# An encoder trunk on one core: the pooling projection third in the mixer, the Fourier projection up, the first gate/up pairs laid out by hand, and RMSNorm factors as columns

## The chip, the cores and the metric

The kernel runs on one core of a Trainium2 chip. Five engines of that core work side by side, each through its own instructions in order: PE (TensorE, matrix products into PSUM), DVE (VectorE), ACT (ScalarE), POOL (GpSimd) and SP (SyncE, which here only issues transfers). They wait for one another by semaphores. The metric is the device time of one execution in microseconds (us), as the median of three runs.

## What is computed

The reference is a two-layer bidirectional encoder on x of 512 positions by 1024 channels in float32:

```python
for l in range(2):
    x = x + 0.5 * swiglu(rmsnorm(x, g1), w_gate, w_up, w_down)      # hidden width 2816
    p = rmsnorm(x, g2) @ w_in          # 256 pool, 256 Fourier, 3 x 512 attention channels
    y_pool = mean pooling (windows 2, 4, 8, 16) minus the token, a 64x64 map per group, a scale
    y_four = Re(fft2 over positions and 64 channels of a group) @ fourier_w
    y_attn = softmax(q1 k1 + alibi) v - lam * softmax(q2 k2 + alibi) v, RMSNorm per head
    x = x + concat(y_pool, y_four, y_attn) @ w_out
    x = x + 0.5 * swiglu(rmsnorm(x, g3), ...)
return rmsnorm(x, g_final)
```

## The kernel before

**Tiling.** x lies transposed in SBUF as eight tiles `x0` to `x7`, 128 channels by 512 positions. Each fp32 product is made of three fp32r matmuls (`mm3`: high x high, high x low, low x high), since a value is kept as a high part `hi` (rounded by ACT) and a low part `lo` (the rest, by DVE); `split` (L102 to L104) makes both. Weights come in as `st` tiles of 512 KB on SP's queue; `operand` hands out the next pair `hi`, `lo`, always AHEAD = 3 operands early, and numbers them in the order of use (`hi139` is the high part of operand 139).

**The feed-forward parts.** 22 row blocks are worked in 11 units of two. A `Unit` is a 2x2 block product by seven products instead of eight (Strassen's scheme in Winograd's form), so its weights and inputs are sums: some sums of weights are made by a second, accumulating transfer on POOL's queue into an `st` tile that has been split already. `head` makes the products `qe` and `qa`, `middle` `qb`, `qg`, then `y`, `v` and `w` (L436 to L438) on DVE and the rest of `qa`, and waits for the norm's factor; `tail`, called after the next unit's head, adds a product to `qg` once `w` has read it, and another to `qe`. A `dn` product per channel tile follows after every 4, 4 and 3 units. The very first unit is a `FirstUnit`: it makes all eight products, as it starts from plain tiles that are there early; the lines that call `plain` for it stand at the end of `build` (L819 to L828).

**Norms.** The products run on x times the gain (`xh`, `xl`), and each result is multiplied by the factor 1/rms later. For the factor, ACT squares the eight tiles, POOL adds six of the squares up (L288), DVE the last; a matmul with ones adds over the partitions (`total`), and nine DVE instructions of 128x512 (`rsqrt`) make the factor, the same in all partitions. The last norm (`Final`) does it otherwise: `columns` has four one-column matmuls give the sums of 4 x 128 positions as a 128x4 tile, the nine instructions run on 128x4, and `dg` (diagonal blocks) with four matmuls spreads the factor over the partitions (`r`, L387).

**The mixer.** Steps named in the string `ORDER` run as listed there: `P0` to `P3` (query and key projections), `N` (factor), `E0` to `E3` (their splits), `Shq` (scores of head h, block q: a max on DVE, an exponential on ACT, a combination on DVE), `T` (transposes), `V0`, `V1`, `VE` (values), `X`, `Y` (attention output), `A` and `F` (pooling and Fourier projections), `AE0`, `AE1` (window sums on DVE), `PD`, `PL0`, `PL1` (pooling maps on PE), `FE0`, `FE1` (folds of the Fourier half on DVE), `FG`, `FD`, `TB`, `GH` (its maps), `W0a` to `W3` (output projection). Each engine's list is a single queue: an instruction that waits holds up all that is behind it on that engine. A scheduler may move instructions of different steps past each other; the lists that result are shown below.

## Time and profile before

| | |
|---|---|
| median of three runs | 1855.18 us (1854.42 to 1856.44) |
| profiled execution, its own time | 1856.4 us |
| its span in the trace | 1854.4 us |
| busy PE, DVE, ACT, POOL | 1767.0, 1314.8, 884.8, 250.0 us |
| mean granted TensorE clock | 0.986 |

The span runs from the first to the last instruction of the trace; 2.0 us of the execution lie around it. PE is busy for 95% of it, so what can be changed by another order is the time in which PE waits, the time in which it runs at half the clock, and the work that it is given. The trace tells of each instruction its start, its length and, in brackets, how long its engine stood idle before it and what ended that.

### The profile page before, as it was taken

What the parts mean: (1) busy time and instruction counts of PE and PEld (TensorE: products, weight loads), DVE (VectorE), ACT (ScalarE), POOL (GpSimd) and SP (SyncE); (2) the same over time, 40 slices, a digit from 0 to 9 for tenths busy, and PEclk for the clock granted to TensorE, in tenths of its full rate; (3) what the DMA queues carried; (4) which work ended last, traced back from release to release, by engine and by line L of the source; (5) the groups of instructions that cost most, each with busy time, mean ns of one, the idle gap of its engine ahead of it and who ended that gap; (6) DMA issues with size and microseconds to landing.
All of it is one profiled execution on the core that took longest, in us unless ns stands there. A gap on an engine that the chain in (4) does not pass through costs nothing.

```text
span 1854.4 us, 28082 instructions
## 1 busy us (share of the span) xinstructions
PE 1767.0 (95%) x11249; PEld 1600.8 (86%) x11249; DVE 1314.8 (71%) x1962; ACT 884.8 (48%) x1225; POOL 250.0 (13%) x272
## 2 busy tenths in 40 slices
PE   7899999999798999999989999999987989999997
PEld 7889989877677889989889899898776888899896
DVE  6865856878679774856898467477877897567474
ACT  6433524468656433524554244244975554244243
POOL 1101101111103101101130010102111210010101
PEclk9899999999999999999999999999999999999998
DMA  8656857454625757857578586675444566586561
GB/s 250 146 159 152 202 137 165 142 139 126 143 65 131 174 152 160 202 138 165 155 156 206 127 197 167 135 173 160 116 118 106 106 147 186 125 195 170 132 164 46
DMA packets 81347, 279.70 MB, mean 151 GB/s; under 512 B 9152, under 2 KB 12224, under 8 KB 81216
## 3 DMA queue, kind: packets, MB, share of 16 engines
q0 software_dynamic: 29376, 106.97, 33.2%
q1 hardware_dynamic: 48672, 167.26, 27.7%
q10 hardware_dynamic: 3168, 3.68, 0.6%
q8 instruction: 88, 1.44, 0.3%
q14 instruction: 43, 0.35, 0.1%
HBM read 258.99 MB, written 2.10 MB: 141 GB/s over the span
## 4 chain that ended last, share of the span: by engine, by line
PE 77%; DVE 8%; ACT 6%; DMA 5%; issue 2%; POOL 0%; SPq 0%; ACTq 0%; DVEq 0%; POOLq 0%
PE dn L107 8%; PE dn L108 7%; PE dn L109 7%; PE qg L420 4%; DMA st<-in_gu 4%; PE qg L421 4%; PE qg L422 4%; PE qe L420 4%; PE qe L421 4%; PE qe L422 4%; PE qa L422 4%; PE qa L421 4%; PE qa L420 4%; DVE lo L104 2%; PE qb L421 2%
## 5 line engine op out<-in xcount | busy, mean ns | idle before, releaser
L103 ACT ACTIVATE hi<-st 128x1024 fp32r<-128x1024 f32 (+2 forms) x420 | 433.1, 1036 | 645.7 <-PE dn L108 218.1
L104 DVE TENSOR_TENSOR lo<-st,hi 128x1024 fp32r<-128x1024 f32 (+2 forms) x420 | 503.5, 1202 | 182.9 <-ACT hi L103 179.8
L108 PE MATMUL dn<-al,hi 128*128 128x512 f32 x704 | 274.6, 390 | 0.0
L109 PE MATMUL dn<-ah,lo 128*128 128x512 f32 x704 | 274.1, 389 | 0.0
L107 PE MATMUL dn<-ah,hi 128*128 128x512 f32 x704 | 272.0, 392 | 0.6
L420 PE MATMUL qg<-xh,hi 128*128 128x256 f32 x688 | 197.4, 287 | 8.7 <-DVE w L438 7.6
L181 POOL DMA_DIRECT2D st<-in_gu x129 | 116.1, 900 | 648.9 <-DVE lo L104 558.5
L421 PE MATMUL qg<-xh,lo 128*128 128x256 f32 x688 | 196.7, 286 | 0.0
L422 PE MATMUL qg<-xl,hi 128*128 128x256 f32 x688 | 196.7, 286 | 0.0
L420 PE MATMUL qe<-xh,hi 128*128 128x256 f32 x608 | 173.4, 285 | 14.5 <-ACT xh L103 8.0
L518 DVE SCALAR_TENSOR_TENSOR x<-dn,x 128x512 f32<-128x512 f32 x96 | 66.2, 689 | 164.7 <-PE dn L109 164.6
L421 PE MATMUL qe<-xh,lo 128*128 128x256 f32 x608 | 172.5, 284 | 2.1 <-DVE lo L104 2.1
L422 PE MATMUL qe<-xl,hi 128*128 128x256 f32 x608 | 172.3, 283 | 1.9 <-DVE xl L104 1.8
L107 PEld LDWEIGHTS dn<-ah,hi 128*128 128x128 f32 x704 | 131.3, 188 | 32.5 <-ACT ah L103 6.5
L108 PEld LDWEIGHTS dn<-al,hi 128*128 128x128 f32 x704 | 132.2, 188 | 28.7 <-DVE al L104 2.4
L109 PEld LDWEIGHTS dn<-ah,lo 128*128 128x128 f32 x704 | 132.2, 188 | 26.7
L420 PEld LDWEIGHTS qg<-xh,hi 128*128 128x128 f32 x688 | 134.0, 195 | 9.5 <-DVE w L438 8.0
L421 PEld LDWEIGHTS qg<-xh,lo 128*128 128x128 f32 x688 | 134.1, 195 | 0.0
L422 PEld LDWEIGHTS qg<-xl,hi 128*128 128x128 f32 x688 | 134.0, 195 | 0.0
L420 PEld LDWEIGHTS qe<-xh,hi 128*128 128x128 f32 x608 | 116.7, 192 | 17.8 <-ACT xh L103 8.8
L420 PE MATMUL qa<-xo,hi 128*128 128x256 f32 x424 | 121.0, 285 | 5.4 <-ACT q L429 5.4
L422 PE MATMUL qa<-xo,hi 128*128 128x256 f32 x424 | 121.3, 286 | 2.8 <-DVE xo L104 2.8
(270 smaller groups left out, 4099.9 us busy)
## 6 DMA issues: line engine op xcount, KB each, us to landing
st<-in_gu SPq DMA_DIRECT2D x176, 512.0 KB, 4.5
st<-in_gu POOLq DMA_DIRECT2D x172, 512.0 KB, 5.6
st<-in_dn SPq DMA_DIRECT2D x64, 512.0 KB, 3.9
lo<-st POOLq DMA_DIRECT2D x32, 512.0 KB, 5.2
st<-in_dn SPq DMA_DIRECT2D x32, 384.0 KB, 3.2
st<-in_qk SPq DMA_DIRECT2D x16, 512.0 KB, 3.7
st<-in_wo SPq DMA_DIRECT2D x16, 512.0 KB, 3.7
st<-in_wv SPq DMA_DIRECT2D x8, 512.0 KB, 4.4
```

The source lines that it names most:

```text
L103: A.activation(hi, src, AF.Copy)
L104: (lo_eng or V).tensor_tensor(lo, src, f(hi), SUB)
L107: T.matmul(o, lh, rh, start=start, stop=False)
L108: T.matmul(o, lh, rl, start=False, stop=False)
L109: T.matmul(o, ll, rh, start=False, stop=stop)
L181: G.dma_start(t[:, 0:w], then, accum_op=ADD)
L420: T.matmul(o, wh[:, s], xh, start=start and p == 0 and z == 0, stop=False, **k)
L421: T.matmul(o, wl[:, s], xh, start=False, stop=False, **k)
L422: T.matmul(o, wh[:, s], xl, start=False, stop=stop and p == NK - 1 and z == 1, **k)
L518: V.scalar_tensor_tensor(X[m], b, 0.5, X[m], MUL, ADD)
```

## The change

- `ORDER`: projection `A` is now third (after `P1`), its window sums `AE0`, `AE1` follow `E0`, `E1` and `P2`, and `PD`, `PL0`, `PL1` lie among the scores. `F` takes the old place of `A` (after `Y1`), and `FE0`, `FE1` come ahead of the scores `S31`, `S33`; `FG0` and `FG1` both come ahead of `W1a`.
- All norms: the squares are added by DVE alone. The factor is made on 128x4 columns as in `Final`, and spread over the partitions by one fp32 matmul of 512 columns (`spread`; ACT copies it to SBUF). In the mixer the spread stands inside `P1`, after 24 of its 48 matmuls, and `VE` takes the columns as they are, so the four transposes `rb` go. `Final` spreads by the one matmul too.
- The first two units: `begin` lists them by hand. The first weights come in four parts, interleaved with the plain tiles; half of the even x tiles come on ACT's transfer queue; the second unit begins with `qa` on an operand that needs no sum (the recipes change for it), then `qe`, `qg`, `qb`; the squares stand after the sums; the first unit's first results are copied out of PSUM. Eight warming matmuls instead of five.

```diff
@@ -50,10 +50,10 @@
 SLOPES = [2.0 ** (-8.0 * (h + 1) / NH) for h in range(NH)]
 NT = S // 2 + 2
 NG = 54
-NWARM = 5
+NWARM = 8
 ORDER = (
-    "P0 N L P1 E1 P2 E0 S01 S11 S13 E2 V0 S03 S00 S10 S12 S22 S02 S21 T0 V1 GD VE TD T1 X0 S23 S20 Y0 P3 "
-    "T2 PD X1 E3 Y1 A GH S30 S32 AE0 AE1 F PL0 X2 S31 S33 PL1 FE0 T3 W0a FE1 Y2 FG0 W1a FG1 TB X3 FD1 FD0 "
+    "P0 N L P1 A E0 E1 AE0 P2 AE1 S01 S11 S13 E2 PD V0 S03 S00 S10 PL0 S12 S22 S02 PL1 S21 T0 V1 GD VE TD T1 X0 "
+    "S23 S20 Y0 P3 T2 X1 E3 Y1 F GH S30 S32 FE0 FE1 X2 S31 S33 T3 W0a Y2 FG0 FG1 W1a TB X3 FD1 FD0 "
     "Y3 W0b W1b W2 W3"
 ).split()
...
@@ -140,6 +140,11 @@
                             continue
                         t, t11 = raw(a21, plus=a22), raw(a11)
                         t12, t22 = raw(a12), raw(a22)
+                        if u == 1 and i == 0:
+                            for x, then in ((t11, a21), (t, a11), (t11, None), (t, a12), (t12, None)):
+                                operand_of(x, then=then)
+                            tail = [(t22, None), (t, None)]
+                            continue
...
@@ -196,10 +209,10 @@
         sm = cp.tile([P, NSMALL], F32, name="sm")
         nc.sync.dma_start(sm, small)
         X = [cp.tile([P, S], F32, name=f"x{k}") for k in range(KT)]
-        load(1)
+        load(1, NK)
         for c in range(2):
             for k in range(0, KT, 2):
-                nc.sync.dma_start(X[k][:, c * TH : (c + 1) * TH], xt[k][:, c * TH : (c + 1) * TH])
+                (nc.sync if c else nc.scalar).dma_start(X[k][:, c * TH : (c + 1) * TH], xt[k][:, c * TH : (c + 1) * TH])
         load(2)
...
@@ -265,9 +277,27 @@
             T.matmul(b, ones, lo, start=False, stop=True)
             return b
 
+        one = cp.tile([P, 1], F32, name="one")
+        V.memset(one, 1.0)
+
+        def columns(sq):
+
+            b = bank("ss")
+            for i in range(4):
+                T.matmul(b[:, i : i + 1], sq[:, i * P : (i + 1) * P], one, start=True, stop=True)
+            return b[:, 0:4]
+
+        def spread(y):
+
+            r, dg = bank("r"), g(name="dg")
+            for i in range(4):
+                V.tensor_scalar(dg[:, i * P : (i + 1) * P], ident, y[:, i : i + 1], None, MUL)
+            T.matmul(r, onef, dg, start=True, stop=True)
+            return r
+
         class Norm:
             def __init__(self, c):
-                self.c, self.h, self.l, self.acc, self.r = c, {}, {}, None, None
+                self.c, self.h, self.l, self.acc, self.col, self.r = c, {}, {}, None, None, None
 
             def feed(self, k):
...
@@ -279,19 +309,34 @@
                 V.tensor_scalar(self.h[k], X[k], gain, None, MUL)
                 V.scalar_tensor_tensor(self.l[k], X[k], gain, f(self.h[k]), MUL, SUB)
 
-            def squared(self, k, eng=G):
+            def square(self, k):
                 sq = g(name="sq")
                 A.activation(sq, X[k], AF.Square)
+                return sq
+
...
                     self.acc = sq
                 else:
-                    (V if k == KT - 1 else eng).tensor_tensor(self.acc, self.acc, sq, ADD)
+                    V.tensor_tensor(self.acc, self.acc, sq, ADD)
+
+            def squared(self, k):
+                self.add(self.square(k))
+
+            def factor(self):
+                v = col(4, "nv", 2)
+                V.tensor_scalar(v, columns(self.acc), -0.5 / D, -0.5 * EPS, MUL, ADD)
+                self.col = rsqrt_of(v, False, 4)
+
+            def spread(self):
+                self.r = g(name="r")
+                A.activation(self.r, spread(self.col), AF.Copy)
 
             def end(self):
                 if self.r is None:
-                    hi, lo = g(F32R), g(F32R)
-                    split(self.acc, hi, lo)
-                    self.r = rsqrt(total(hi, lo), D, False)
+                    if self.col is None:
+                        self.factor()
+                    self.spread()
 
         class PairNorm(Norm):
...
+
+            def second(self, k):
+
+                gain = sm[:, self.c + k : self.c + k + 1]
+                hi, lo = g(F32R, name="xh"), g(F32R, name="xl")
+                A.activation(hi, X[k], AF.Copy, scale=gain)
+                V.scalar_tensor_tensor(lo, X[k], gain, f(hi), MUL, SUB)
+                for c in range(2):
+                    s = slice(c * TH, (c + 1) * TH)
+                    self.x[k // 2][2 + c] = hi[:, s], lo[:, s]
 
...
@@ -432,12 +474,17 @@
                 self.qb, self.qg = bank("qb"), bank("qg")
                 self.product(self.qb, 6, True, True)
                 self.product(self.qg, 7, True, True)
+                self.combine()
+
+            def combine(self, then=None, ahead=True):
                 self.y, self.v, self.w22 = g(name="y"), g(name="v"), g(name="w22")
                 V.tensor_tensor(self.y, self.qb, self.q1, ADD)
                 V.tensor_tensor(self.v, self.qe, self.y, ADD)
                 V.tensor_tensor(self.w22, self.qg, self.v, SUB)
-                self.product(self.qa, 2, False, True)
+                self.product(self.qa, 2, False, True, ahead=ahead)
                 self.nm.end()
+                if then:
+                    then()
                 r = self.nm.r
                 self.r = [r[:, i * TH : (i + 1) * TH].unsqueeze(1).to_broadcast([P, 2, TH]) for i in range(2)]
                 self.t = [halves(wide("t")) for _ in range(2)]
...
@@ -497,11 +531,59 @@
                     res.append(self.hidden(t))
                 return res
 
+        def begin(nm, act):
+
+            with tc.manual_schedule():
+                produce(0, NK, lambda j: nm.plain(2 * j, 0))
+                for k in range(0, KT, 2):
+                    nm.plain(k, 1)
+                produce(1)
+                for k in range(1, KT, 2):
+                    nm.second(k)
+                pos[2] = 2
+                upto(4)
+                one, two = FirstUnit(nm), Unit(nm)
+                c0, c1 = one.head(), one.head()
+                for x in nm.x.values():
+                    del x[0]
+                nm.sums(0)
+                for i in range(2):
+                    q, c0[i] = c0[i], g(name="c")
...
+                nm.sums(1)
+                upto(5)
+                nm.sums(2)
+                upto(6)
+                nm.sums(3)
+                two.qa, two.qe, two.qg, two.qb = bank("qa"), bank("qe"), bank("qg"), bank("qb")
+                two.product(two.qa, 1, True, True, ahead=False)
+                two.product(two.qe, 5, True, True, ahead=False)
+                sq = [nm.square(k) for k in range(KT)]
+                two.q1 = g(name="q1")
+                A.activation(two.q1, two.qa, AF.Copy)
+                upto(7)
+                two.product(two.qg, 7, True, True, ahead=False)
+                for x in sq:
+                    nm.add(x)
+                upto(8)
+                nm.factor()
+                two.product(two.qb, 6, True, True, ahead=False)
+                upto(9)
+                two.combine(lambda: upto(10), ahead=False)
+                upto(11)
+                act += one.tail([c0, c1])
+            return two
+
         def ffn(nm, nxt, first=False):
             for c0, c1 in CHUNKS:
                 act, last = [], None
                 for u in range(c0, c1):
-                    unit = FirstUnit(nm) if first and u == 0 else Unit(nm)
+                    if first and u == 0:
+                        first, last = None, begin(nm, act)
+                        continue
+                    if first is None and u == 1:
+                        continue
+                    unit = Unit(nm)
                     unit.head()
                     if last:
...
-            def proj():
+            def proj(between=None):
                 w = weights()
                 b = [bank("pp0"), bank("pp1")]
-                pair(b, w, nm.h, nm.l)
+                pair(b, w, nm.h, nm.l, between=between)
...
 
             def do_values_out():
-                rb = bank("rb")
-                for i in range(4):
-                    T.transpose(rb[:, i * P : (i + 1) * P], nm.r[:, i * P : (i + 1) * P], ident)
-                rcol = col(4, "rcol", 2)
-                V.tensor_copy(rcol, rb[:, 0:S:P])
+                rcol = nm.col
...
-                "N": nm.end, "L": do_lam, "V0": lambda: do_values(0), "V1": lambda: do_values(1), "VE": do_values_out,
+                "N": nm.factor, "L": do_lam, "V0": lambda: do_values(0), "V1": lambda: do_values(1), "VE": do_values_out,
...
             for n in ("P0", "P1", "P2", "P3", "A", "F"):
-                steps[n] = lambda n=n: bk.__setitem__(n, proj())
+                steps[n] = lambda n=n: bk.__setitem__(n, proj(nm.spread if n == "P1" else None))
```

On ACT at the start, around the squares of the first norm (`sq`), before:

```order
L103 ACTIVATE hi6_449<-st4_109 128x1024
L347 ACTIVATE xg_49_320<-x6_87,sm_79 128x512
L347 ACTIVATE xg_50_321<-x7_88,sm_79 128x512
L103 ACTIVATE hi7_527<-st5_172 128x1024
L103 ACTIVATE xh_53_330<-ta_51_324 128x512
L103 ACTIVATE xh_55_334<-tb_52_325 128x512
L103 ACTIVATE hi8_557<-st6_206 128x1024
L284 ACTIVATE sq_57_502<-x0_81 128x512
```

and now:

```order
L314 ACTIVATE sq_69_567<-x6_87 128x512
L314 ACTIVATE sq_70_569<-x7_88 128x512
L563 ACTIVATE q1_71_571<-qa_59_503 128x512
L103 ACTIVATE hi6_573<-st5_182 128x1024
L103 ACTIVATE hi7_608<-st4_112 128x1024
L103 ACTIVATE hi8_656<-st6_204 128x1024
L333 ACTIVATE r_79_690<-r_80_691 128x512
L103 ACTIVATE hi9_704<-st8_452 128x1024
```

Operands 6, 7 and 8 stood ahead of the eight squares, and now stand behind them.

On DVE in the second feed-forward part of layer 0, at the end of the second unit's `middle` (`w22` is the `w` of the text above), before:

```order
L104 TENSOR_TENSOR lo138_6165<-st100_5772,hi138_6164 128x1024
L104 TENSOR_TENSOR al_739_6026<-t_729_5888,ah_738_6025 128x512
L436 TENSOR_TENSOR y_742_6096<-qb_740_6029,q1_733_5951 128x512
L437 TENSOR_TENSOR v_743_6097<-qe_731_5892,y_742_6096 128x512
L104 TENSOR_TENSOR lo139_6196<-st101_5804,hi139_6195 128x1024
L438 TENSOR_TENSOR w22_744_6098<-qg_741_6030,v_743_6097 128x512
```

and now:

```order
L481 TENSOR_TENSOR y_745_6117<-qb_743_6050,q1_736_5972 128x512
L482 TENSOR_TENSOR v_746_6118<-qe_734_5913,y_745_6117 128x512
L104 TENSOR_TENSOR lo138_6186<-st100_5786,hi138_6185 128x1024
L483 TENSOR_TENSOR w22_747_6119<-qg_744_6051,v_746_6118 128x512
L492 TENSOR_TENSOR t_749_6152<-w22_747_6119,r_729_5900 128x2x256
L104 TENSOR_TENSOR lo139_6217<-st101_5818,hi139_6216 128x1024
```

`lo139` stood ahead of `w22`, and now stands behind it. In layer 1 the same pair (`lo365` and `w22`) changes places in the same way.

On DVE in the mixer of layer 0, ahead of the maxes of score `S31` (`ISA sc,mx<-S3`), before:

```order
L104 TENSOR_TENSOR g_554_4992<-m_542_4893,g_553_4991 128x512
L686 TENSOR_TENSOR m_546_4910<-m_546_4910,pad_545_4906 128x8 x2
L698 TENSOR_SCALAR yp_556_4999<-PL_555_4995,sm_79 128x512
L104 TENSOR_TENSOR yl_558_5002<-yp_556_4999,yh_557_5001 128x512
L565 ISA sc_568_5031,mx_563_5024<-S3_567_5028,al_112 128x512
```

and now:

```order
L782 TENSOR_TENSOR ft_573_5049<-pp1_540_4910,r_300_3903 128x512
L786 MEMSET e_574_5050 128x1
L783 TENSOR_TENSOR e_574_5050<-ft_573_5049 128x255
L784 TENSOR_TENSOR e_574_5050<-ft_573_5049 128x255
L785 COPY e_574_5050<-ft_573_5049 128x1
L787 COPY zf1_141<-ft_573_5049 128x1
L104 TENSOR_TENSOR el_576_5058<-e_574_5050,eh_575_5057 128x512
L104 TENSOR_TENSOR zl_578_5062<-zf1_141,zh_577_5061 128x128
L647 ISA sc_588_5091,mx_583_5084<-S3_587_5088,al_115 128x512
```

The windows and the map `PL` stood there; now the two folds (`FE1` is shown) do.

## Rows read from the trace of the kernel before

**Rows 1.** The page: shares of the chain of work that ended last, by engine.

```profile
PE 77%; DVE 8%; ACT 6%; DMA 5%; issue 2%; POOL 0%; SPq 0%; ACTq 0%; DVEq 0%; POOLq 0%
```

**Rows 2.** The start on PE, timeline: start in us, length in us, instruction, and in brackets the idle time before it and what ended it.

```profile
7.64 0.58 PE L420 MATMUL qc<-xo,hi 128*128 128x256 f32 x1 [2.81 <-ACT xo L338]
...
41.10 0.58 PE L420 MATMUL qe<-xh,hi 128*128 128x256 f32 x1 [3.59 <-ACT xh L103]
...
50.05 0.58 PE L420 MATMUL qa<-xo,hi 128*128 128x256 f32 x1 [5.35 <-ACT q L429]
```

**Rows 3.** The start by stretches: from:to, length, busy time and instructions of PE, PEld, DVE, ACT, POOL, then granted clock, DMA share, GB/s.

```profile
7.60:13.30 5.70, 5.66 (x26) 5.62 (x27) 3.81 (x10) 4.40 (x10) 0.00 (x0) 1.00 0.94 306
...
37.50:57.80 20.30, 10.77 (x48) 10.08 (x48) 15.93 (x23) 10.88 (x18) 2.59 (x3) 0.66 0.61 131
57.80:72.10 14.30, 11.67 (x96) 11.29 (x95) 13.16 (x19) 7.78 (x10) 0.86 (x1) 1.00 0.44 98
```

**Rows 4.** The start on ACT and DVE, timeline: the eight squares and the copy of `qa` on ACT; the seven adds and a low part on DVE.

```profile
45.27 4.25 ACT L284 ACTIVATE sq<-x 128x512 f32<-128x512 f32 x8
49.43 0.57 ACT L429 ACTIVATE q<-qa 128x512 f32<-128x512 f32 x1
...
46.54 5.46 DVE L288 TENSOR_TENSOR sq<-sq,sq 128x512 f32<-128x512 f32 x7
51.92 1.22 DVE L104 TENSOR_TENSOR lo<-st,hi 128x1024 fp32r<-128x1024 f32 x1
```

**Rows 5.** The second feed-forward part on PE and DVE, timeline: the waits of `qg` for `w` in layer 0 and in layer 1, and what DVE did in the first of them.

```profile
629.89 0.58 PE L420 MATMUL qg<-xh,hi 128*128 128x256 f32 x1 [4.20 <-DVE w L438]
...
1536.77 0.58 PE L420 MATMUL qg<-xh,hi 128*128 128x256 f32 x1 [3.40 <-DVE w L438]
...
628.01 1.23 DVE L104 TENSOR_TENSOR lo<-st,hi 128x1024 fp32r<-128x1024 f32 x1 [4.43 <-ACT hi L103]
629.15 0.69 DVE L438 TENSOR_TENSOR w<-qg,v 128x512 f32<-128x512 f32 x1
```

**Rows 6.** The stretch behind the wait of layer 0 and the one after it, columns as in rows 3.

```profile
627.74:634.57 6.83, 4.68 (x22) 4.68 (x23) 2.52 (x3) 0.73 (x2) 0.00 (x0) 0.50 0.31 89
634.57:641.40 6.83, 6.83 (x59) 6.83 (x59) 6.25 (x8) 5.18 (x6) 1.43 (x2) 1.00 0.37 88
```

**Rows 7.** Norms: one of the nine narrow DVE instructions of the last norm and its successor, and the diagonal blocks; on PE its four one-column matmuls and its spread (timeline); then, as groups with busy time and mean ns, the first half of the sum of a wide norm and the transposes `rb`.

```profile
1842.07 0.16 DVE L250 TENSOR_TENSOR t<-y 128x4 f32<-128x4 f32 x1
1842.26 0.16 DVE L254 TENSOR_TENSOR t<-t,v 128x4 f32<-128x4 f32 x1
...
1843.44 0.88 DVE L386 TENSOR_SCALAR dg<-ident,y 128x128 f32<-128x128 f32 x4
...
1838.97 0.95 PE L374 MATMUL ss<-one,sq 128*128 128x1 f32 x8
...
1843.78 2.08 PE L387 MATMUL r<-dg,onef 128*128 128x128 f32 x8 [2.15 <-DVE dg L386]
...
L264 PE MATMUL ss<-g,ones 128*128 128x512 f32 x6 | 2.8, 460 | 0.6 <-ACT g L103 0.6
...
L645 PE MATMUL rb<-ident,y 128*128 128x128 f32 x8 | 1.2, 273 | 0.0
```

**Rows 8.** The adds of squares on POOL (group), and two like DVE instructions (timeline), the first while POOL adds, the second while it does not.

```profile
L288 POOL TENSOR_TENSOR sq<-sq,sq 128x512 f32<-128x512 f32 x30 | 47.2, 1575 | 77.0 <-ACT sq L284 76.1
...
572.87 2.35 DVE L316 TENSOR_TENSOR ta<-xg 128x256 f32<-128x256 f32 x1
...
568.46 0.41 DVE L317 TENSOR_TENSOR ta<-xg,xg 128x256 f32<-128x256 f32 x1
```

**Rows 9.** The mixer of layer 0 from the second half of `P2` to the values, by stretches, columns as in rows 3.

```profile
396.70:408.70 12.00, 11.54 (x51) 9.21 (x50) 8.62 (x13) 11.48 (x18) 0.86 (x1) 1.00 0.57 129
408.70:432.00 23.30, 22.57 (x95) 17.78 (x96) 20.32 (x67) 22.60 (x45) 4.01 (x4) 1.00 0.48 126
```

**Rows 10.** The end of the same mixer on PE, timeline: the waits around the pooling maps `PL`, then the stretch at a lower clock (columns as in rows 3).

```profile
503.51 0.50 PE L107 MATMUL PL<-g,g 128*128 128x512 f32 x1 [3.04 <-ACT g L103]
...
506.98 0.80 PE L108 MATMUL PL<-g,g 128*128 128x512 f32 x1 [2.51 <-DVE g L104]
...
515.47 0.50 PE L107 MATMUL PL<-g,g 128*128 128x512 f32 x1 [1.48 <-ACT g L103]
...
517.77 0.50 PE L107 MATMUL wo<-yh,hi 128*128 128x512 f32 x1 [0.84 <-DVE yp L698]
...
504.86:511.69 6.83, 4.71 (x11) 3.79 (x12) 3.54 (x11) 0.63 (x1) 0.00 (x0) 0.50 0.86 224
```

**Rows 11.** Lengths on DVE and ACT at that place, timeline: a max of a score, a combination, an exponential, the fold's product, its sum and its low part.

```profile
494.81 0.68 DVE L565 CUSTOM_DVE_ANT_0 sc<-S,al 128x512 f32<-128x512 f32 x1
500.24 0.74 DVE L580 SCALAR_TENSOR_TENSOR sc<-sc,rc,sc 128x512 f32<-128x512 f32 x1
...
497.60 0.71 ACT L570 ACTIVATE sc<-sc,nb 128x512 f32<-128x512 f32 x1
...
519.15 0.68 DVE L704 TENSOR_TENSOR ft<-pp,y 128x512 f32<-128x512 f32 x1
520.40 0.42 DVE L705 TENSOR_TENSOR e<-ft 128x255 f32<-128x255 f32 x1
521.92 0.69 DVE L104 TENSOR_TENSOR el<-e,eh 128x512 fp32r<-128x512 f32 x1 [0.63 <-ACT eh L103]
```

More of the change, by code (lines that the diff above doesn't have):

```diff
@@ L152, in build, with load @@
         pos = [0, 0, 0]
-        def load(upto):
+        def load(upto, parts=1):
             while pos[1] < min(len(raws), upto):
@@ L157, in load @@
                 st = stp.tile([P, 1024], F32, tag="st", name=f"st{pos[1]}")
-                nc.sync.dma_start(st[:, 0:w], src)
+                q = w // parts
+                for j in range(parts):
+                    nc.sync.dma_start(st[:, j * q : (j + 1) * q], src[:, j * q : (j + 1) * q])
                 if plus is not None:
@@ L162, in load, with produce @@
                 pos[1] += 1
-        def produce(i, parts=1):
+        def produce(i, parts=1, between=None):
             src, w, eng, then = recipes[i]
@@ L391, in finish, with pair @@
                     (nc.sync if k % 2 else nc.scalar).dma_start(out[k], t)
-        def pair(b, w, rh, rl, ks=range(KT), steps=((0, 4), (4, 7), (7, 8))):
+        def pair(b, w, rh, rl, ks=range(KT), steps=((0, 4), (4, 7), (7, 8)), between=None):
             w0h, w0l, w1h, w1l = w
             order = [(k, z) for q in steps for z in range(2) for k in range(*q) if k in ks]
-            for k, z in order:
+            for n, (k, z) in enumerate(order):
+                if between and n == 8:
+                    between()
                 wh, wl = (w0h, w0l) if k < 4 else (w1h, w1l)
@@ L410, in __init__, with product @@
                 self.nm = nm
-            def product(self, q, j, start, stop, w=None):
-                wh, wl = w or operand()
+            def product(self, q, j, start, stop, w=None, ahead=True):
+                wh, wl = w or operand(ahead)
                 k = {"skip_group_check": True}
```

75 lines of the change are left out of this document (23 added, 52 removed).

## The prediction

> **What bounds the kernel now.** PE does. The page's chain of waits [rows 1] puts 77% of the span on it, and the table has it busy for 1767 of 1854.4 us. So I looked for the other 87 us: first the timeline of PE for its waits of over a third of a microsecond, then the windows around each for the clock and for what the other engines did, and last the lists of instructions, for what now stands ahead of the instruction that PE waited for. Three kinds of place came out. The start: 7.64 us pass before the first product [rows 2], the first 26 take 0.22 us each, and from 37.5 to 57.8 us PE makes 48 products in 20.3 us [rows 3]. The second feed-forward part of each layer: one wait of 4.20 and one of 3.40 us [rows 5]. The end of each mixer: four waits around the pooling maps [rows 10]. A product of 256 columns takes 6.83 / 59 = 0.116 us where the clock is whole, and about 4.68 / 22 = 0.213 where the granted clock is 0.50 of 2.4 GHz, that is 1.2 [rows 6]. Those low stretches follow long waits, so such a wait costs more than its length.
>
> **The second feed-forward parts: about -12 us.** In layer 0 DVE finished `v`, then stood for 4.43 us until ACT had `hi139`, made `lo139` (1.23 us) and only then `w`, for which PE's `qg` waited [rows 5]. `lo139` had nothing to do with `w`; it stood ahead of it. Now `w` comes first. From the end of `y` and `v` nothing is late any more, so the 4.20 us go. The products behind the wait ran at half the clock from 629.89 to 634.57, 22 of them [rows 5, 6]; at 0.12 they take 2.6 instead of 4.7 us: 2.0 more. What is late next is `lo139` itself, for the `qg` of the third unit: between lie 24 + 20 + 24 products, 68 x 0.12 = 8.2 us; counted from where the wait begins, 629.89 - 4.20 = 625.69, PE comes to it at 633.9, and `lo139` was there at 629.24. So no new wait, as long as the transfer into its `st` tile is no later. Layer 1: 3.40, and some 2.3 for the clock by the same reckoning (an estimate). Together 6.2 + 5.7 = 12. Bounds: nothing at all, if the transfer is later by some 5 us (it hangs on buffers that come free earlier or later), and 14.
>
> **The start: about -5 us.** Gains: the first weights and x tiles come in parts on two queues, so that the first product may begin near 6.7 instead of 7.64; some 0.5 to 1.5 us more from the early products at 0.22 us. The two waits of 3.59 and 5.35 us [rows 2] vanish as such: `qe` no longer follows the first products directly, and `qa`, which had waited for a copy behind the eight squares [rows 4], has no such copy ahead of it. New waits, as the lists show: operands 6 to 8 now stand behind the squares on ACT, so `qg` waits for `hi6` and `lo6` (about 1 us for the rest of 4.25 us of squares, then 1.06 and 1.22); `ss` waits for the seven adds on DVE, 5.46 us [rows 4], of which the products of `qg` hide 2.9, so 3; `lo7` and `lo8` behind them, about 1; the spread waits for `y` to `w` and the diagonal blocks, and `hi9` stands behind the copy of `r` on ACT: 3 with what the clock loses. Against 14.5 us lost from 37.5 to 57.8 (20.3 less 48 x 0.12) and 2.8 from there to 72.1 (14.3 less 96 x 0.12), 17 in all [rows 3], that is some 11. PE gets 0.95 for the columns and up to 2.08 for the spread [rows 7], where it had two sums of 0.46. So -1 - 1.5 (early products, taken at the upper end) - 6 + 2.1 = -6.4; I take -5, since every step of a chain written by hand has to hold. Bounds -11 and +2.
>
> **The norms elsewhere.** Nine wide instructions (0.69 each, as `w` [rows 5]) become nine narrow ones of about 0.195 from start to start, plus 0.88 for the blocks [rows 7]: on DVE 6.0 becomes 2.7. The adds leave POOL: 30 of them, 1.58 us each, beside which the same subtraction on DVE took 2.35 instead of 0.41 us [rows 8]. Six adds of 0.69 on DVE are 4.1 us; what they replace, 1.94 us of stretch for one such pair, is of that order in a norm, so DVE loses nothing. On PE a norm costs 0.95 + 2.08 instead of 2 x 0.46 [rows 7], +2.1, and I know no cover for it, as PE is the bound; it is 2.1 in each of the five norms behind the start. In the two feed-forward parts of that kind and the one of layer 1's beginning this is paid back by the earlier factor and the unhindered DVE (small waits for it stand at the beginning of each such part): 0, between -2 and +2 each.
>
> The Trainium skill (SBUF — State Buffer, Who interferes with whom) says that a DVE instruction with two SBUF inputs and a GpSimd instruction that reads SBUF lock each other out for a whole instruction. The rows of 2.35 and 0.41 us agree: the slow one is about the fast one plus one POOL add. By that rule DVE would gain all 47.2 us of POOL's adds and not the part taken here; as PE is the bound, the sum would move by no more than a microsecond a norm.
>
> The Trainium skill (VectorE: DVE Perf Modes, The TRN2 errata) speaks against the columns: an SBUF instruction pays a fixed cost however small it is, so work should be in tiles of 512 elements or more. The rows agree that 128x4 at 0.16 us is no 128th of 128x512 at 0.69; but it is under a quarter of it. By that rule the columns would bring less than their size suggests, and the sum stays.
>
> **The mixers: about +2 us each.** PE: +2.1 for the norm, less the four transposes (1.2 us for two layers [rows 7], 0.6): +1.5. The scores: ahead of them PE has now `A` too, 48 products of 0.23, so the first scores wait no longer for their splits (0.8 of the 1.2 us that PE stands idle in [rows 9], by their two lines 12.00 - 11.54 and 23.30 - 22.57). But PL0, PL1 and PD move among them, where ACT is busy for 22.60 of 23.30 us and DVE for 20.32 [rows 9]; two maps cost some 2.5 us on ACT and 4.5 on DVE. `E0`, `E1` are earlier by what `A` takes, which frees as much. I take +1, between -1 and +4.
> The end: the four waits of 3.04, 2.51, 1.48 and 0.84 go, 7.9 us, with about 2.2 for the low clock until 511.69 (4.7 us of it, in which 11 products of 0.23 ran) [rows 10]. In their place PE waits for DVE. From the start of `GH` PE has 12 x 0.12 + 8 x 0.23 (scores) + 12 x 0.23 (values) + 8 x 0.23, 7.8 us of work up to the transposes T3. DVE needs 3.8 us for the two splits behind `GH`, then 2.6 for four maxes, two combinations of 0.74, two folds of about 2.7 (0.68 + 2 x 0.42 + 0.69 and small ones), then the maxes of S31 [rows 11], and the last transposes of S30 need PSUM banks that only these maxes free: 3.8 + 10.9 = 14.7. So a wait of 6.9, then 2.5 us of work, then about 1 until S31 has gone through its exponentials (0.71 each) and its combination; with 2 for the clock 10, against 10.1 now. The place is another and the sum is nought, between -4 and +6. Each mixer: 1.5 - 0.8 + 1 + 0 = +1.7, say +2.
>
> **The end of the kernel:** one spread that waits for all four blocks instead of four that follow one another: +0.4.
>
> **Sum.** -12 - 5 + 4 + 0.4 = -12.6, against the profiled execution of 1856.4 us (its span of 1854.4 and 2.0 around it): 1843.8. That execution is 1.2 above the median of 1855.18, so the forecast is 1842.6, say **1842.5 us**.
>
> **The rivals.**
> The wait for the transfer comes back. Both feed-forward waits would only move from `w` to `lo139`, if the loads are as late as PE is early. For it: the 4.43 us in which DVE stood ahead of `lo139` show how late that load was. Against it: the 8.2 us of products between. Then some +10: 1852.
> The mixers lose. The mechanism is the fold ahead of S31: `FE0` and `FE1` (5.4 us) lie between PE and all of the last head, and PE has nothing else in its list there. If DVE comes to the folds late by 8 us, because the maps pushed its work in the scores back, each mixer loses 9 more: 1842.5 + 18 = 1860.5. It decides from some 8 us more per mixer. For it: DVE and ACT are at 87 and 97% in the scores [rows 9]; against it: PE stands for only 1.2 us there now, and `E0` and `E1` leave that stretch.
> The mixers gain. If T3 waits less than 4 us and the clock stays whole, each gives 7 more: 1828.5.
> The start brings nothing, since the hand-written order has as many waits as the old: 1847.5.
>
> **Chances.** Forecast 0.49; transfer 0.15 (half of it inside 0.2%); mixers lose 0.13; mixers gain 0.15; no gain at the start 0.08. The bound of 0.2%, about what a measurement of this kernel can tell, is 3.7 us, so 1851.5 to 1858.9 is no change. Faster 0.49 + 0.15 + 0.08 + 0.05 = 0.77, same 0.10, slower 0.13. The range leaves out the slower case and the lowest part of the last gain: 1828 to 1856.
>
> **What would show it.** Right: no wait for `w` near 621 to 630 and 1533, full clock there; the second unit's `qg` at the start (72.06 now) near 66 to 68; in each mixer a wait ahead of T3 of 6 to 8 us in place of the waits for `PL`; the products `ss` and `r` at about 1 and 2 us. Wrong: a wait for `lo139`; waits inside the scores of over 2 us in sum; T3 later than 12 us behind the last score; more stretches of low clock than now.

## The result and the profile after

The changed kernel took 1843.25 us (median of 4 runs, 1842.39 to 1845.28), the kernel before 1855.81 (4 runs beside it, 1854.42 to 1856.87): ratio 0.9934, 95% interval 0.9917 to 0.9952. The profiled execution took 1843.82 us, its span 1842.0. Here and below, single runs far outside the rest (4479.85 us once with `e8_spread_twice`, 2909.64 once with `e3_pool_adds`, 1951.19 and 4887.81 with the kernel before) are left out of medians and ratios. The total came out as forecast; its parts did not. To see that, both spans are cut where the same products begin: at the first product of `P0` (374.76 us before, 367.50 after, in layer 0), at the first `qe` behind a mixer (573.46 and 572.10), at the first product behind the first run of `dn` (156.65 and 149.40), and at the first `ss` behind the last run (1838.97 and 1825.77).

| stage, us | before | after | difference | forecast |
|---|---|---|---|---|
| start, to the end of the first `dn` run | 156.65 | 149.40 | -7.25 | -5 |
| mixer 0 | 198.69 | 204.61 | +5.9 | +2 |
| second part, layer 0, to its first `dn` run | 140.08 | 131.35 | -8.7 | -6.2 |
| first part, layer 1, to its first `dn` run | 132.21 | 132.94 | +0.7 | 0 |
| mixer 1 | 199.07 | 204.72 | +5.7 | +2 |
| second part, layer 1, to its first `dn` run | 139.90 | 130.27 | -9.6 | -5.7 |
| end, behind the last `dn` run | 15.40 | 16.28 | +0.9 | +0.4 |

The rest of the feed-forward parts took the same time in both. The differences add up to -12.4; the spans differ by 12.3. For comparison, the kernel before in another profiled execution had 155.65, 200.31, 137.97, 131.90, 198.96 and 140.03 in the first six rows, the changed one 150.46, 204.47, 130.02, 129.76, 204.88 and 130.49. So a stage scatters by 1 to 3 us from one execution to the next.

The page of after: busy time, share and instructions of each engine.

```profile
PE 1773.6 (96%) x11286; PEld 1605.9 (87%) x11286; DVE 1280.7 (70%) x2004; ACT 886.4 (48%) x1223; POOL 204.8 (11%) x242
```

PE is busy for 6.6 us longer in a shorter span. More work, or the same at a lower clock? That has to be read by stage.

**The second feed-forward part.** The place of [rows 5] on DVE, then the same stretch on PE (timeline, layer 0).

```profile
617.11 0.69 DVE L482 TENSOR_TENSOR v<-qe,y 128x512 f32<-128x512 f32 x1
617.72 1.22 DVE L104 TENSOR_TENSOR lo<-st,hi 128x1024 fp32r<-128x1024 f32 x1
618.85 0.68 DVE L483 TENSOR_TENSOR w<-qg,v 128x512 f32<-128x512 f32 x1
...
621.93 1.23 DVE L104 TENSOR_TENSOR lo<-st,hi 128x1024 fp32r<-128x1024 f32 x1 [1.68 <-ACT hi L103]
```

```profile
619.42 0.28 PE L462 MATMUL qe<-xh,hi 128*128 128x256 f32 x1
619.59 0.39 PE L462 MATMUL qg<-xh,hi 128*128 128x256 f32 x1
```

`w` now comes straight behind `v` and a low part that was ready, and PE goes from `qe` to `qg` without a bracket, where 4.20 us stood. In layer 1 the longest wait of the stage is now one of 1.58. The low part that comes late (it waits for ACT until 621.93) stands behind `w`, and no product waits for it. The windows say the same of the clock: whole from 600 to 635, where [rows 6] had a stretch at 0.50. One such stretch is left in the part, at 590.7, behind waits of under 2 us.

```profile
572.10:600.00 27.90, 25.27 (x189) 24.16 (x188) 22.66 (x44) 14.98 (x22) 3.49 (x4) 0.94 0.67 150
600.00:635.00 35.00, 35.00 (x293) 34.91 (x292) 28.53 (x35) 20.64 (x24) 5.20 (x6) 1.00 0.85 191
```

**The start.** Windows of after, at the places of [rows 3], then PE's timeline (places of [rows 2], and the waits in between).

```profile
7.10:12.80 5.70, 5.70 (x49) 5.66 (x49) 4.10 (x10) 4.65 (x10) 0.00 (x0) 1.00 0.93 324
37.00:57.80 20.80, 14.22 (x88) 12.49 (x89) 14.37 (x29) 8.03 (x12) 1.99 (x3) 0.92 0.37 84
```

```profile
7.17 0.28 PE L462 MATMUL qc<-xo,hi 128*128 128x256 f32 x1
...
39.83 0.38 PE L462 MATMUL qg<-xh,hi 128*128 128x256 f32 x1 [3.01 <-ACT hi L103]
...
41.09 0.55 PE L463 MATMUL qg<-xh,lo 128*128 128x256 f32 x1 [0.88 <-DVE lo L104]
...
46.14 1.02 PE L287 MATMUL ss<-one,sq 128*128 128x1 f32 x8 [0.53 <-DVE sq L321]
...
56.03 0.38 PE L462 MATMUL qe<-xh,hi 128*128 128x256 f32 x1 [1.63 <-ACT hi L103]
56.98 0.38 PE L462 MATMUL qa<-xo,hi 128*128 128x256 f32 x1 [0.56 <-ACT hi L103]
...
64.40 0.28 PE L462 MATMUL qg<-xh,hi 128*128 128x256 f32 x1
```

The first 5.7 us hold 49 products instead of 26, and the 20 us from 37 hold 88 instead of 48. The second unit takes up `qg` again at 64.40. That is the 361st feed-forward product; before, the 361st began at 70.70, and the `qg` that the prediction names, at 72.06, was the one behind it. The largest wait left behind the first product is one of 3.01.

**The mixer.** PE's timeline in layer 0: the new waits, and below them two of the three stretches at half the clock (columns as in [rows 3]; the third is 498.55 to 501.96).

```profile
449.49 0.80 PE L107 MATMUL PL<-g,g 128*128 128x512 f32 x1 [5.10 <-ACT g L103]
...
497.88 0.51 PE L107 MATMUL GH<-g,g 128*128 128x256 f32 x2 [3.21 <-ACT g L103]
...
507.10 0.40 PE L645 MATMUL S<-kl,qs 128*128 128x512 f32 x1
507.34 0.38 PE L670 MATMUL T<-ident,sc 128*128 128x128 f32 x2
510.16 0.33 PE L670 MATMUL T<-ident,sc 128*128 128x128 f32 x1 [2.44 <-DVE ft L782]
513.22 0.47 PE L670 MATMUL T<-ident,sc 128*128 128x128 f32 x1 [2.73 <-DVE mx L647]
```

```profile
447.35:454.17 6.82, 4.68 (x13) 3.42 (x14) 4.63 (x11) 3.78 (x10) 1.56 (x2) 0.50 0.40 92
...
512.20:519.02 6.82, 5.67 (x16) 4.40 (x17) 5.67 (x21) 4.40 (x11) 1.26 (x1) 0.50 0.00 0
```

The waits of [rows 10] are gone. In their place come 2.44 and 2.73 ahead of the last transposes, as announced but shorter, and also 5.10 among the scores. Ahead of `GH`, where PE had waited 1.98 us before (1.23 in the other execution), it now waits 3.21. For the 5.10, ACT's timeline: the product's high part (`g`, at 448.82) stands behind six exponentials, a high part and a scaling from 442.77 on, while PE has run out at 449.49 - 5.10 = 444.39.

```profile
448.12 0.71 ACT L652 ACTIVATE sc<-sc,nb 128x512 f32<-128x512 f32 x1
448.73 0.19 ACT L652 ACTIVATION_READ_ACCUMULATOR sc<-sc,nb 128x1 f32 x1
448.82 0.61 ACT L103 ACTIVATE g<-m 128x512 fp32r<-128x512 f32 x1
```

To tell waiting from clock, the table has for each stage the sum of PE's gaps, then half of its busy time in stretches at 0.50 (what the same work would not have taken at full clock); what is left is work.

| gaps / lost to the clock / work, us | mixer 0 | mixer 1 | second part, layer 0 | layer 1 |
|---|---|---|---|---|
| before | 16.3 / 2.4 / 180.1 | 16.3 / 2.7 / 180.0 | 10.4 / 2.3 / 127.4 | 9.9 / 2.9 / 127.1 |
| before, other execution | 14.9 / 5.5 / 179.9 | 16.2 / 2.7 / 180.1 | 9.0 / 1.7 / 127.3 | 10.2 / 2.7 / 127.2 |
| after | 17.6 / 6.9 / 180.1 | 18.4 / 5.9 / 180.4 | 2.6 / 1.6 / 127.1 | 2.7 / 0 / 127.5 |
| after, other execution | 18.8 / 5.4 / 180.4 | 18.3 / 6.1 / 180.5 | 2.6 / 0 / 127.4 | 2.8 / 0 / 127.7 |

A mixer has the same work, about 2 us more waiting and about 3 us more at the low clock. In the first pair the second parts lost 7 to 8 us of gaps, of which only 4.20 and 3.40 were the waits for `w`.

### The profile page after: what moved, and what is told of

It reads as the page before. It is cut to its first block, busy times and chain, and to the rows that moved or that the text cites. A ratio compares the mean times of both kernels' runs of the same rounds, so it can differ in the third digit from the quotient of the medians.

```text
span 1842.0 us, 28151 instructions
## 1 busy us (share of the span) xinstructions
PE 1773.6 (96%) x11286; PEld 1605.9 (87%) x11286; DVE 1280.7 (70%) x2004; ACT 886.4 (48%) x1223; POOL 204.8 (11%) x242
## 5 line engine op out<-in xcount | busy, mean ns | idle before, releaser
L462 PE MATMUL qe<-xh,hi 128*128 128x256 f32 x688 | 197.2, 287 | 4.2 <-DVE nv L328 2.3
L464 PE MATMUL qe<-xl,hi 128*128 128x256 f32 x688 | 195.6, 284 | 1.1 <-DVE xl L104 1.1
L463 PE MATMUL qe<-xh,lo 128*128 128x256 f32 x688 | 195.5, 284 | 0.0
L462 PEld LDWEIGHTS qe<-xh,hi 128*128 128x128 f32 x688 | 132.6, 193 | 8.2 <-ACT hi L103 4.9
L462 PEld LDWEIGHTS qg<-xh,hi 128*128 128x128 f32 x688 | 134.0, 195 | 5.1 <-ACT hi L103 3.2
L464 PEld LDWEIGHTS qe<-xl,hi 128*128 128x128 f32 x688 | 132.7, 193 | 1.3 <-DVE xl L104 1.3
L463 PEld LDWEIGHTS qe<-xh,lo 128*128 128x128 f32 x688 | 132.6, 193 | 1.3 <-issue 0.7
```

The source lines that it names most:

```text
L462: T.matmul(o, wh[:, s], xh, start=start and p == 0 and z == 0, stop=False, **k)
L463: T.matmul(o, wl[:, s], xh, start=False, stop=False, **k)
L464: T.matmul(o, wh[:, s], xl, start=False, stop=stop and p == NK - 1 and z == 1, **k)
```

## The experiments

Each ratio is against the kernel before on the same chip.

**What put `w` first, and what it gave: `e2_wide_factor` and `e3_pool_adds`.** The first makes the factor on 128x512 again in all norms but the very first and the last; the second gives six of the seven adds of squares back to POOL in the same norms. (The last norm has its six adds on POOL in every version, 8.9 us.)

```diff
 def factor(self):
+    if self.c == C_FFN1:
...
+        return
+    hi, lo = g(F32R), g(F32R)
+    split(self.acc, hi, lo)
+    self.r = rsqrt(total(hi, lo), D, False)
...
-self.add(self.square(k))
+self.add(self.square(k), V if k == KT - 1 else G)
```

> The changed kernel with the factor of all norms but the first made wide again (sum by two fp32r matmuls, nine instructions of 128x512, four transposes in the mixer); DVE still adds the squares. Theory: the narrow factor is what let w come ahead of the late low part on DVE in the second feed-forward parts; so the waits of 4 and 3 us return with their low clock, and each second feed-forward part (131.4 and 130.3 us to its second down projection's end) grows by 4 to 6 us, while the mixers and the other norms lose about 2 us of PE work: the kernel at 1843 to 1848. Rival: the adds moved from POOL to DVE are what freed those parts: they stay at 130 to 132, and with less work for PE the kernel falls to about 1836.

> The changed kernel with six of the seven adds of squares back on POOL in all norms but the first. Theory: the adds matter only for the small waits at the beginnings of the feed-forward parts: each of three parts grows by 1 to 3 us, the waits for w do not return, the kernel at 1846 to 1850. Rival: beside POOL's adds DVE is late enough that the old waits return in full: 1855. Second rival: DVE has room, no change: 1843.

The wide factor took 1850.21 us, ratio 0.9970 (0.9957 to 0.9983). PE's timeline in both layers shows the waits again; the second parts took 134.7 and 137.6, 3.4 and 7.4 more than after. The mixers took 202.8 and 202.1, 1.8 and 2.6 less than after, with 179.2 and 179.3 us of work on PE.

```profile
623.35 0.51 PE L468 MATMUL qg<-xh,hi 128*128 128x256 f32 x1 [2.34 <-DVE w L489]
...
1530.08 0.58 PE L468 MATMUL qg<-xh,hi 128*128 128x256 f32 x1 [4.00 <-DVE w L489]
```

On DVE, the late low part is ahead of `w` once more.

```profile
621.47 1.23 DVE L104 TENSOR_TENSOR lo<-st,hi 128x1024 fp32r<-128x1024 f32 x1 [2.57 <-ACT hi L103]
622.61 0.68 DVE L489 TENSOR_TENSOR w<-qg,v 128x512 f32<-128x512 f32 x1
```

With the adds on POOL the ratio was 0.9971 (0.9958 to 0.9985), 1850.07 us. Here `w` stays ahead and PE does not wait for it. The second parts take 134.0 and 133.1, about 3 more, of which 1.7 and 2.2 are small waits at their beginning (gaps of 4.3 and 4.9 instead of 2.6 and 2.7), such as these.

```profile
575.80 0.39 PE L462 MATMUL qe<-xh,hi 128*128 128x256 f32 x1 [0.77 <-ACT xh L103]
...
579.56 0.39 PE L464 MATMUL qe<-xl,hi 128*128 128x256 f32 x1 [1.24 <-DVE xl L104]
```

So the two edits have separate effects. The narrow factor let the scheduler put `w` ahead. Of the small waits each took about half: without those for `w`, gaps were 6.2 and 6.5 before and are 2.6 and 2.7 after; 4.0 and 4.3 are left with the wide factor, 4.3 and 4.9 with the adds on POOL. What the adds change on DVE, the group of one subtraction shows (busy time, mean ns), first of after, then with the adds back: 420 ns on average become 794; in the kernel before it was 1027.

```profile
L361 DVE TENSOR_TENSOR ta<-xg 128x256 f32<-128x256 f32 x16 | 6.7, 420 | 0.9 <-ACT xg L401 0.9
```

```profile
L361 DVE TENSOR_TENSOR ta<-xg 128x256 f32<-128x256 f32 x16 | 12.7, 794 | 0.9 <-ACT xg L401 0.9
```

**The start: `e4_old_start`.** The kernel before, with the new norms and the new `ORDER`, and its own first two units.

> The kernel before with the new step order and the new norms, but the first two units as before. Theory: the start's gain is a stage of its own: 7.3 us longer up to 156 us, all later stages as in the changed kernel: 1850.5. Rival: the start's gain comes partly from the first factor made narrow, which this kernel has too: then 4 or less, 1847 or lower.

Measured 1844.66, ratio 0.9941 (0.9925 to 0.9957), which the rival had expected (1847 or lower). In the profiled execution the start took 153.93: 4.5 more than the hand-written one in after, 2.7 less than before. That would give 4.5 of the 7.25 to the new beginning and the rest to the norm, but the division is not firm, since the hand-written start took 149.40 to 153.88 in the eleven profiled executions that have it. The beginning itself is clearer: its 361st product starts at 63.61 to 65.93 in these eleven, at 69.48 in `e4`, at 70.70 and 69.70 in the two executions of before. What of this reaches the total is not shown: its median is 1.4 and 2.0 us above those of the changed kernel, and the intervals overlap.

**The mixer's order: `e1_old_order`.** The line `ORDER` of the kernel before, all else as changed.

```diff
-    "P0 N L P1 A E0 E1 AE0 P2 AE1 S01 S11 S13 E2 PD V0 S03 S00 S10 PL0 S12 S22 S02 PL1 S21 T0 V1 GD VE ...
+    "P0 N L P1 E1 P2 E0 S01 S11 S13 E2 V0 S03 S00 S10 S12 S22 S02 S21 T0 V1 GD VE ...
```

> The changed kernel with the old step order in the mixer (norms and start as changed). Theory: the new step order is what makes each mixer 5.7 to 5.9 us longer than before, by the wait for the second pooling map among the scores (5.1 us and the low clock behind it); the factor's products are only about 1.5 of it. Then each mixer takes about 200.5 us instead of 204.6, and the kernel about 1835. Rival: the factor's products on PE and the spread inside P1 are the price, and the order is neutral: mixers stay at 204 to 205 and the kernel at 1843.

Measured 1839.61, ratio 0.9922 (0.9902 to 0.9942), the lowest of all, though the interval overlaps with that of the changed kernel. The mixers took 201.4 and 201.9, 3 less than after in each. Their gaps were 15.1 and 15.4 instead of 17.6 and 18.4; the time lost to the clock stayed at 5.4 and 5.6. So the new `ORDER` costs about 3 us of waiting per mixer. The other 2.5 are there with the old `ORDER` too, as low clock. Its waits (PE's timeline) are nearly those of [rows 10]: 3.04, 1.82 and 1.45.

```profile
498.71 0.80 PE L107 MATMUL PL<-g,g 128*128 128x512 f32 x1 [3.04 <-ACT g L103]
...
502.19 0.80 PE L108 MATMUL PL<-g,g 128*128 128x512 f32 x1 [1.82 <-DVE g L104]
...
511.17 0.51 PE L107 MATMUL PL<-g,g 128*128 128x512 f32 x1 [1.45 <-ACT g L103]
```

**Can the waits be moved away? `e5_maps_late`, `e6_folds_late`, `e7_f_last`, `e10_cover`.** Four orders: the maps behind the scores of head 2, the folds behind the last scores, `F` behind the last scores with the maps as in the first and the folds and table loads (`TD`) behind T3, and the same with the maps behind `E3`.

```diff
e5
-S10 PL0 S12 S22 S02 PL1 S21 T0 V1 GD VE
+S10 S12 S22 S02 S21 T0 V1 PL0 PL1 GD VE
e6
-GH S30 S32 FE0 FE1 X2 S31 S33 T3
+GH S30 S32 X2 S31 S33 FE0 FE1 T3
e7
-Y1 F GH S30 S32 FE0 FE1 X2 S31 S33 T3 W0a
+Y1 GH S30 S32 X2 S31 S33 F T3 TD FE0 FE1 W0a
e10, against e7
-T0 V1 PL0 PL1 GD VE T1 X0 S23 S20 Y0 P3 T2 X1 E3 Y1
+T0 V1 GD VE T1 X0 S23 S20 Y0 P3 E3 PL0 PL1 T2 X1 Y1
```

> The changed kernel with the pooling maps PL0 and PL1 moved from among the scores to behind the second half of the values (V1). Theory: the wait of 5.1 us for the second map's high part, which stands on ACT behind the exponentials, and the low clock behind it, are the price of the maps among the scores: each mixer falls from 204.6 to about 199 and the kernel by 10 to 1833. Rival: at that place PE would wait for the scores anyway (their combinations are done only 5 us later too), so the wait goes over to the transposes T0: the mixers stay above 203 and the kernel at 1840 to 1843.

> The changed kernel with the folds FE0 and FE1 behind the scores S31 and S33. Theory: the two waits ahead of the transposes T3 (2.4 and 2.7 us, with low clock behind them) come from the folds ahead of the maxes on DVE: they fall to 2 us or less in sum, each mixer 3 us shorter, the kernel at about 1837. Rival: the last head's own chain of max, exponential and combination fills the same time, as PE has nothing else there: mixers within 1 us of 204.6, the kernel unchanged.

> The changed kernel with the maps behind V1, the projection F between the scores S31, S33 and the transposes T3, the folds behind T3, and the loads of the tables behind T3 (buffers). Theory: F is 11 us of PE work that waits for nothing, so it covers the last head's chain, and the maps cost nothing behind V1: all waits of over 2 us in the mixer go but the one ahead of GH, mixers at 195 to 198 us, the kernel at 1826 to 1832. Rival: the waits move on to the fold's maps FG or to the tables' late loads: mixers above 200, the kernel at 1835 or more.

> The changed kernel with the maps behind P3, E3 right behind P3, the projection F between S31, S33 and the transposes T3, the folds and the tables' loads behind T3. Theory: each of the three waits of over 2 us is one for a chain on ACT and DVE that needs PE work beside it; P3 covers the maps, F covers the last head, so only GH keeps a wait of about 3; mixers at 196 to 199, the kernel at 1828 to 1834. Rival: as with F last, the wait goes over to GH or S30, which then have no projection beside them: mixers at 203 or more.

| | median, us | ratio | mixers, us |
|---|---|---|---|
| after (`e11_after`) | 1842.69 | 0.9929 (0.9911 to 0.9946) | 204.5, 204.9 |
| `e5_maps_late` | 1843.03 | 0.9943 (0.9930 to 0.9956) | 205.2, 204.9 |
| `e6_folds_late` | 1848.81 | 0.9965 (0.9952 to 0.9978) | 207.0, 207.2 |
| `e7_f_last` | 1852.34 | 0.9982 (0.9970 to 0.9995) | 207.3, 206.8 |
| `e10_cover` | 1858.19 | 1.0007 (0.9996 to 1.0019) | 210.2, 210.6 |

None gained. PE's timeline of `e5`, `e6`, `e7` and `e10` in layer 0 shows where each wait went.

```profile
450.73 0.59 PE L107 MATMUL PL<-g,g 128*128 128x512 f32 x1 [3.02 <-ACT g L103]
...
455.02 0.79 PE L107 MATMUL PL<-g,g 128*128 128x512 f32 x1 [2.03 <-ACT g L103]
```

```profile
528.64 0.39 PE L107 MATMUL FG<-g,eh 128*128 128x256 f32 x1 [2.80 <-DVE tl L104]
```

```profile
499.99 0.58 PE L107 MATMUL GH<-g,g 128*128 128x256 f32 x1 [10.70 <-ACT g L103]
```

```profile
477.36 0.79 PE L105 MATMUL PL<-g,g 128*128 128x512 f32 x1 [7.31 <-ACT g L101]
...
500.66 0.58 PE L105 MATMUL GH<-g,g 128*128 128x256 f32 x1 [8.52 <-ACT g L101]
```

In `e5` the 5.10 for one map became 3.02 + 2.03 for two. In `e6` the waits ahead of T3 shrank to 1.35 and 1.70, and `FG` waited 2.80, by its row for a low part of the transposes (`tl`), which was done at 528.6; the last low part of the folds was done at 526.75. In `e7` the waits ahead of T3 were gone, and `GH`, which had lost the products of `F` ahead of it, waited 10.70. In `e10` the maps waited where they were put, and `GH` still 8.52.

**Is it the wait or its clock? `e9_fill`.** Products on data that is there, whose result is never read, ahead of three of the waits: 20 ahead of `PL1`, 13 ahead of `GH`, 10 each ahead of the first and last transposes of head 3.

```diff
+def fill(b, x, n):
+    for _ in range(n):
+        T.matmul(b, ones, x, start=True, stop=True)
```

> The changed kernel with matmuls of ones that nobody reads, laid where PE waits in the mixer: 20 ahead of the second pooling map, 13 ahead of GH, twice 10 ahead of the transposes T3 (512 columns each, into the bank that the real product then overwrites). Theory: three stretches at 1.2 GHz behind these waits cost each mixer 6 to 7 us, 3 to 4.5 more than before the change, and that, not longer waiting, is why the mixers grew; with PE kept at work the stretches go, the mixers fall to 200 or 201, the kernel to about 1834. Rival: the clock is not decided by these waits, or the fills come late into the real work: mixers at 204 or more.

Measured 1845.52, ratio 0.9945 (0.9925 to 0.9965); mixers 205.6 and 205.3. Gaps fell to 9.1 and 10.1 and the loss to the clock to 4.5 and 3.0, but PE's work rose by 12, to 192.1 and 192.3. What the fills saved they cost. The last of them also missed its wait: by its row it waited 2.73 us for the same max itself and began behind it. And the clock still fell, as PE's timeline and the window show: behind a wait of 1.34 among transposes.

```profile
446.48 4.82 PE L771 MATMUL PL<-xh,ones 128*128 128x512 f32 x20
...
455.74 1.27 PE L672 MATMUL T<-ident,sc 128*128 128x128 f32 x8 [1.34 <-DVE mx L647]
...
515.65 3.87 PE L771 MATMUL T<-yh,ones 128*128 128x512 f32 x9 [2.73 <-DVE mx L647]
```

```profile
457.56:464.38 6.82, 5.58 (x20) 4.50 (x21) 6.07 (x13) 5.57 (x12) 0.00 (x0) 0.50 0.94 216
```

**What the spread costs: `e8_spread_twice`.** The spread's matmul is issued twice.

```diff
 T.matmul(r, onef, dg, start=True, stop=True)
+T.matmul(r, onef, dg, start=True, stop=True)
```

> The changed kernel with every spread matmul (ones times the diagonal blocks, fp32, 512 columns) done twice. Theory: PE has no room for the factor's products, so each of the six norms and the last grows by the 1.9 to 2.1 us of one spread: 1843 + 11 to 14, the mixers at 206.6. Rival: the spread falls into time in which PE waits anyway: 3 us or less in all.

Measured 1846.66, ratio 0.9957 (0.9942 to 0.9972), 3.4 above after and so between what the theory and its rival expected. The profiled span was 1844.9, 2.9 above that of after; the mixers took 204.9 and 205.3, at most 0.6 more, and the end 17.97, 1.7 more. PE's timeline in mixer 0 gives the price without any difference of runs.

```profile
385.89 1.02 PE L295 MATMUL r<-dg,onef 128*128 128x512 f32 x2
386.75 1.02 PE L296 MATMUL r<-dg,onef 128*128 128x512 f32 x2
```

From one start to the next it is 0.86 us, for two instructions of the trace, so 0.43 each.

**The two kernels again: `e11_after` and `e12_before`.** Unchanged, as a measure of the scatter.

> The changed kernel itself once more, on the chip of the two others, so that stages are compared within one chip: 1843, mixers within 1 us of 204.6 and stretches at 1.2 GHz at the same three places.

> The kernel before, profiled once more on another chip. Theory: the stretches at 1.2 GHz belong to the order of work, so its mixers again take 198.5 to 199.5 us and lose 2 to 3 us each to the clock, against 5 to 7 in the changed kernel. Rival: the stretches fall as chance has it: then the mixers differ from the first profile by 2 us or more.

The changed kernel gave 1842.69 and a ratio of 0.9929 (0.9911 to 0.9946), as at first. The kernel before gave 1854.71 in one run; its mixer 0 lost 5.5 us to the clock, its mixer 1 2.7 (table above). So the low clock of one mixer varies by 3 us between executions of one kernel. The mixers of the changed kernel lay at 5.4 to 6.9 in all four cases.

## Why the prediction came out right, and where its terms did not

**The second feed-forward parts (-12, measured -18.3).** The mechanism is shown: `w` ahead of the late low part (`e2` undoes it, `e3` does not), the clock with it, and no wait for that low part, so the transfer rival fell. Too small was the term "norms elsewhere", taken as nought: the adds on DVE are worth about 3 us in each of these parts (`e3`), and the narrow factor also took away some 1.5 us of small waits in each (`e2`). By the prediction's reading of the Trainium skill (SBUF — State Buffer, Who interferes with whom), that two such instructions lock each other out, DVE would be freed for all of POOL's adds, 47.2 us. With the adds back DVE is busy for 1293.9 us instead of 1280.7, without 30 adds of its own (20.7 at 0.69): 33.9 us lost beside 48.6 of POOL. So the reading holds in direction and in about 0.7 of its size. That this would move PE by no more than a microsecond a norm, as the prediction had it, was too low for these two parts.

**The start (-5, measured -7.25, -5.2 in the other pair).** The waits came where they were forecast: 3.9 us for `hi6` and its low part (3.3 reckoned), 0.53 for `ss` (3 reckoned), 2.2 for `hi9` and what follows it (3 with the clock). The early products took 0.12. The rival "the start brings nothing" was partly right in another sense: some of the gain, 2.7 in the one execution of `e4`, comes without the hand-written order.

**The norm on PE (+2.1 each).** The spread was priced from a row at half the clock: 2.08 us for eight passes of 128 columns in [rows 7], behind a wait, granted clock 0.50. The one matmul takes 2.08 at that place too, again at 0.50 (row and window below), but 1.02 in the mixer at full clock, and 0.86 from its start to the next. What it replaces was priced too high: the two sums were taken at 0.46 each, the mean length of a row, but lengths of neighbours overlap. From start to start the two take 0.46 together, and the columns 0.81 (PE's timeline of before, then of after).

```profile
385.64 0.39 PE L264 MATMUL ss<-g,ones 128*128 128x512 f32 x1
385.87 0.39 PE L265 MATMUL ss<-g,ones 128*128 128x512 f32 x1
386.10 0.39 PE L107 MATMUL pp<-xh,hi 128*128 128x512 f32 x1
```

```profile
378.38 0.94 PE L287 MATMUL ss<-one,sq 128*128 128x1 f32 x8
379.19 0.49 PE L107 MATMUL pp<-xh,hi 128*128 128x512 f32 x1
```

So a norm is 1.67 against 0.46, +1.2, and less the four transposes (0.6) a mixer has +0.6. The runs show a little more: PE's work in a mixer is 180.9 in both layers of `e1`, 0.8 and 0.9 above the kernel before with the same `ORDER`, and in `e2`, with the wide factor, 0.9 and 1.1 below the changed kernel. That the table has the same work before and after means that the new `ORDER` saves about as much; how is open. The end of the kernel (+0.4, measured +0.9) has the spread at half the clock: there the diagonal blocks are waited for 2.74 us instead of 2.15 [rows 7].

```profile
1831.17 2.08 PE L295 MATMUL r<-dg,onef 128*128 128x512 f32 x2 [2.74 <-DVE dg L294]
```

```profile
1831.17:1833.30 2.13, 2.08 (x2) 0.50 (x2) 0.01 (x1) 0.00 (x0) 0.00 (x0) 0.50 0.00 0
```

**The mixers (+2 each, measured +5.9 and +5.7).** The forecast weighed the right chain at its end. From the start of `GH` (497.88) to the last transposes (513.22), which a max of S31 releases, it took 15.3 us; 14.7 had been reckoned. PE came to T3 later than assumed, 9.5 us after `GH` instead of 7.8, in part at half the clock, and so it waited 5.2 and not 7.9; the last of T3 began 6.1 us behind the last score (507.10 to 513.22), well under the 12 named. So neither mixer rival held by its own mechanism. What was missing were two waits outside this chain: 5.10 for a map among the scores, which the prediction's own test named as a sign of being wrong (over 2 us), and the one ahead of `GH`, which grew from 1.98 to 3.21. Another of its signs came true as well: there are 11 stretches of low clock instead of 7 (9 and 8 in the other pair). What the maps alone cost was not measured, as `e5` moved their wait and gained nothing. `e1` shows about 3 us for the order per mixer. The remaining 2.5 are there with the old order too, as 0.8 to 0.9 of work for the norm and about 3 at the low clock, less about 1 of waiting. What sets the low clock off is open: `e9` took about half of the waiting away, and the clock still fell.

**The sum.** The gains were 25.6 us instead of 17, the losses 13.2 instead of 4.4 (the four terms of the forecast, and the first part of layer 1, which had been put at nought). The total is right because two errors of 8.6 and 8.8 cancel, and it says little for the terms. Whether the old order with the new norms and start is truly faster than the changed kernel can't be told from 1839.61 and 1842.69 with overlapping intervals; that its mixers are shorter by 3 us each, the profiles show.

## What to carry to other kernels

Look in the instruction list for what stands ahead of the waited-for instruction: a late low part had held `w`, and making another chain on that engine shorter was enough to put it behind. Moving a step into a busy stretch moved its wait along: none of four other orders of this mixer gained, and where `F` covered one wait (`e7`), its products were missing ahead of another. Price an instruction only from a row whose granted clock you have read, and compare stage by stage, since errors of over 8 us can cancel in a total.

## What the runs showed of the hardware that was not expected

- The granted clock fell to 0.50 without a long wait: at 590.7 in the second part (behind waits of 1.58 and 0.77 us) and at 457.56 in `e9` after one of 1.34 among transposes. The same two waits in layer 1, and in both layers of `e11_after`, had no such stretch behind them.
- One fp32 matmul of 512 columns stands in the trace as two instructions of 0.43 us from start to start, so spreading four blocks by one instruction took 0.86 at full clock; the fp32r products beside it (`pp`) begin 0.23 after one another.
- Unread products as filler held off part of the low clock (a loss of 3.0 and 4.5 us in a mixer instead of 5.4 to 6.9) and cost all of what it saved (12 us more work).
